# Three partial sums at later turns, and the gain row spread by one-pass products

## The chip, the core and the metric

The kernel runs on one core of one Trainium2 chip. The metric is the time of one execution on the device in microseconds (us). Three timed runs of the kernel before gave 869.16, 869.48 and 869.73 us. A profiled execution, taken separately, is what the views below show.

## What is computed

One encoder layer on a sequence of 512 tokens of width 1024, in float32: an S5 state-space branch and a gated spatial mixer run side by side and are merged by two sigmoid gates; then come attention to 256 memory tokens and a SwiGLU network.

```python
n = rms_norm(h, mix_norm_g)            # h = x
proj = n @ w_in                         # 1024 x 4608: xa, zu, zv, gate_a, gate_b
ya = s5_branch(xa, ...)                 # two scans, GLU with w_glu
yb = sgu_branch(zu, zv, ...)            # layer norm, 128 x 128 mixing per head
merged = sigmoid(gate_a) * (ya @ w_proj_a) + sigmoid(gate_b) * (yb @ w_proj_b)
h = h + merged @ w_out
h = h + memory_cross_attention(rms_norm(h), rms_norm(mem), w_q, w_k, w_v, w_xo)
h = h + (silu(rms_norm(h) @ w_gate) * (rms_norm(h) @ w_up)) @ w_down
return rms_norm(h, final_norm_g)
```

## The kernel before

**Products.** TensorE has a one-pass product for operands of the type float32r and a slower one, which shows as two matmul records, for plain float32. Nearly every matrix product uses the first: each operand is split into a high part (a cast by ScalarE, line 85) and the rest (a subtraction by VectorE, line 86), and three products, high by high, high by rest and rest by high, are added (mm3, line 401). Several large products (gate b, the queries, the SwiGLU network) are done with seven products of half-size blocks instead of eight; these need sums and differences of weight blocks.

**The plan.** All weight blocks, 512 KB each, stand in one list in the order of use. next_w (line 374) is called once for each block, at its *turn*: it starts the loads that are due up to seven turns ahead (begin, line 387; most loads are due three turns ahead, into three buffers named wraw), splits the blocks up to two turns ahead (three buffers each for whi and wlo), and hands out the block of the turn. The turns that matter here: 36 to 49 are the 14 products of gate b, 50 and 51 w_glu, 52 to 55 w_proj_a, 56 to 63 w_out, 64 on w_k.

**The partial sums.** The sums of weight blocks that the queries and w_down need later are made in device memory by transfers alone (plan_sums, line 301). Each is a pair: a copy, issued by SyncE (line 316), and two to four turns later an addition, a GpSimd transfer that adds a second block to the first (line 317). plan_sums is given the turn of each copy and the distance to its addition. The eight pairs of the queries come first; the next seven, at turns 50 to 62, are six chunks of one sum of w_down and the first chunk of another.

**What sets the order.** The kernel is built by a planner that traces the program and then orders each engine's instructions itself, by what is ready first in its own model of time. An instruction named in keep_in_program_order (in_order for short) stays behind the instruction that was traced just before it on its engine. The copies of the partial sums are held in this way; their additions are not.

**The gate stage.** Around turns 36 to 49 the tile gw holds the blocks of gate b's two halves (plan_gates, line 233). ORDER (line 230) is the order of the products (q, i), with q the number of the product and i the half: (1, 0), (1, 1), (2, 0), (2, 1), (5, 0), (6, 0), (5, 1), (7, 0), (6, 1), (4, 0), (7, 1), (3, 0), (4, 1), (3, 1). Once the block of (6, i) is split, a GpSimd transfer adds a further block of w_in to it in place (line 261); the result is the block of (4, i). Products 6, 7 and 4 of a half add up in one bank of TensorE's output memory (gx); between 7 and 4 ScalarE copies the bank out as u (kept, line 1311, line 1313), so product 4 waits for that copy. The four loads named gat (line 1452), the other gate's values, are traced after w_glu and before turn 52.

**The front.** g_row, one row of 1024 numbers on one partition, is the gain of the first norm. It is spread over 128 partitions by products with a row of ones (pg, line 638). idles (line 610) issues products of a tile of ones that nobody reads; they keep TensorE busy ahead of its first real work. row_sums squares a row of x in halves on ScalarE, rms_factor makes r from it on VectorE and GpSimd, scaled multiplies x by r and by pg, then x is transposed by TensorE (line 577) and split.

Of the kernel before, what the change touches and what calls it, by code (L numbers as in the profile page):

```python
# [9 lines left out]
F32 = mybir.dt.float32  # L10
F32R = mybir.dt.float32r
AF = mybir.ActivationFunctionType
ALU = mybir.AluOpType
# [4 lines left out]
P = 128  # L18
D = 1024
# [33 lines left out]
def hybrid_layer_kernel(  # L53
# [8 lines left out]
    nc = tc.nc  # L62
# [17 lines left out]
    def aux(name, shape=(P, 512)):  # L80
        return pa.tile(list(shape), F32, tag="aux", name=name)
# [12 lines left out]
    in_order = tc.keep_in_program_order  # L94
# [119 lines left out]
    def query_block(i, j, n):  # L214
        return block(w_q, i * KD // 2, KD // 2, 512 * n + 256 * j, 256)
# [78 lines left out]
    def down_block(i, jc, c):  # L294
        row, k = (4 * c + 2 * i, 2) if c < CHUNKS - 1 else (NF - 2 + i, 1)
        return block(w_down, row, k, 512 * (1 - jc), 512)

    def down_sum(q, c):
        return dsum[q][:, 2 * c:min(2 * c + 2, NF // 2), :]

    def plan_sums(places):


        jobs = []
        for q, first, more in ((5, (0, 0), lambda n: query_block(0, 1, n)), (7, (0, 1), lambda n: query_block(1, 1, n)),
                               (6, None, lambda n: query_block(1, 1, n)), (4, None, lambda n: query_block(1, 0, n))):
            for n in range(2):
                jobs.append((qsum[q, n], qsum[q + (-1 if q == 6 else 2), n] if first is None else query_block(*first, n),
                             more(n)))
        for q, i, jc, more in ((5, 0, 0, lambda c: down_block(0, 1, c)), (7, 0, 1, lambda c: down_block(1, 1, c)),  # L310
                               (6, 1, 1, lambda c: down_sum(5, c)), (4, 1, 0, lambda c: down_sum(6, c))):
            for c in range(CHUNKS):
                jobs.append((down_sum(q, c), down_block(i, jc, c), more(c)))
        assert len(jobs) == len(places)
        for (dst, src, more), (j, step) in zip(jobs, places):
            plan[j][1].append((0, lambda d=dst, x=src: tc.keep_in_program_order(nc.sync.dma_start(d, x))))
            plan[j + step][1].append((0, lambda d=dst, x=more: nc.gpsimd.dma_start(d, x, accum_op=ALU.add)))  # L317
# [44 lines left out]
    for i in range(4):  # L362
# [4 lines left out]
    plan_down(w_down, lambda q, c: down_tokens[0](q, c), down_plan)  # L367
    plan_units(UNITS, down_plan)

    plan_sums([(5 + 3 * i, 3) for i in range(8)] + [(50 + 2 * i, 2) for i in range(7)] +  # L370
              [(85 + 3 * i, 3) for i in range(3)] + [(122 + 5 * i, 4) for i in range(14)])
    used_w = [0]

# [22 lines left out]
    def split_w(j):  # L396
        tiles.append(plan[j][2]())
# [132 lines left out]
    ones = cp.tile([P, P], F32, name="ones")  # L530
# [10 lines left out]
    def rms_factor(ss, r=None):  # L541

        ms = np_.tile([P, 1], F32, tag="ms", name="ms", bufs=2)
        if r is None:
            r = np_.tile([P, 1], F32, tag="r", name="r", bufs=2)
        nc.vector.tensor_tensor(ms, ss[:, 0:1], ss[:, 1:2], ALU.add)
        nc.vector.tensor_scalar(ms, ms, 1.0 / D, EPS, ALU.mult, ALU.add)
        nc.gpsimd.tensor_tensor(r, ms, mhalf, ALU.pow)
        return r

    HALF = (slice(0, 512), slice(512, 1024))

    def row_sums(src, order=(0, 1)):
        ss = np_.tile([P, 2], F32, tag="ss", name="ss", bufs=2)
        for i in order:
            sum_sq(ss[:, i:i + 1], src[:, HALF[i]])
        return ss
# [13 lines left out]
    def to_feat(src, hi, lo, tsl, full=None, skip=None, part=(0, 1), behind=None):  # L571

        for q in part:
            ps = aux("ptr", (P, 4, P))
            for j in range(4):
                k = 4 * q + j
                tr = nc.tensor.transpose(ps[:, j, :], src[:, k * P:(k + 1) * P], ident)  # L577
                row_tr[0] = tr.ins
                if behind is not None:
                    in_order(tr)  # L580
            if q != skip:
                turned[:] = split(hi[:, 4 * q:4 * q + 4, tsl], lo[:, 4 * q:4 * q + 4, tsl], ps)
            if full is not None:
                nc.scalar.copy(full[:, 4 * q:4 * q + 4, tsl], ps)
        if behind is not None:
            long_idle(*behind)
# [8 lines left out]
    def slot(tag, shape, dt, name):  # L595
        return sp.tile(list(shape), dt, tag=tag, name=name)
# [13 lines left out]
    def idles(n):  # L610
        for i in range(n):
            in_order(nc.tensor.matmul(idle, ones, ones, start=True, stop=True))

    idles(8)
    warm = np_.tile([P, 1], F32, tag="ms", name="warm", bufs=2)
    nc.scalar.activation(warm, mhalf, AF.Square)

# [2 lines left out]
    g_row = np_.tile([1, D], F32, tag="gain", name="g_row", bufs=2)  # L620
# [13 lines left out]
    def first_rows():  # L634

        pg = [aux("pg") for i in range(2)]
        for i in range(2):
            in_order(nc.tensor.matmul(pg[i], ones[0:1, :], g_row[:, HALF[i]], start=True, stop=True))
        idles(1)
        def scaled(t, q, r, g):  # L640
            return in_order(nc.vector.scalar_tensor_tensor(
                xt[:, t, HALF[q]], xt[:, t, HALF[q]], r, g, ALU.mult, ALU.mult))

        def gain_copy(q):
            in_order(nc.vector.tensor_copy(g_mix[:, HALF[q]], pg[q]) if q == 0 else
                     nc.scalar.copy(g_mix[:, HALF[q]], pg[q]))

        def turn(t, q):
            to_feat(xt[:, t, :], xn_hi, xn_lo, slice(t * P, t * P + P), part=(q,))

        def parts(j):
            raw = plan[j][3].pop("raw")
            hi = wp.tile([P, 2, 512], F32R, tag="hi", name="whi", bufs=3)
            lo = wp.tile([P, 2, 512], F32R, tag="lo", name="wlo", bufs=3)
            tiles.append((hi, lo))
            high = lambda q: in_order(nc.scalar.copy(hi[:, q], raw[:, q]))
            low = lambda q: in_order(nc.vector.tensor_tensor(lo[:, q], raw[:, q], hi[:, q].bitcast(F32), ALU.subtract))
            return high, low

        pinned[0] = True  # L660
        r = rms_factor(row_sums(xt[:, 0, :], (1, 0)))
        scaled(0, 0, r, pg[0])
        high, low = parts(0)
        high(0)
        low(0)
        gain_copy(0)
        turn(0, 0)
        idles(3)
        scaled(0, 1, r, pg[1])
        r = rms_factor(row_sums(xt[:, 1, :]))  # L670
        high(1)
        low(1)
        high, low = parts(1)
        wide = slice(0, 2)
        high(wide)
        gain_copy(1)
        scaled(1, 0, r, g_mix[:, HALF[0]])
        low(wide)
        turn(1, 0)
        turn(0, 1)  # L680
        scaled(1, 1, r, g_mix[:, HALF[1]])
        split_w(2)
        ss = row_sums(xt[:, 2, :])
        r = rms_factor(ss)
        turn(1, 1)
        turned1 = [row_tr[0]]
        pinned[0] = False
        with tc.issue_after(turned[0].ins):
            ss = row_sums(xt[:, 3, :])
        for t in range(2, NT):  # L690
            with tc.issue_after(turned[1].ins) if t > 2 else nullcontext():
                for i in range(2):
                    sc = nc.vector.scalar_tensor_tensor(
                        xt[:, t, HALF[i]], xt[:, t, HALF[i]], r, g_mix[:, HALF[i]], ALU.mult, ALU.mult)
            r = rms_factor(ss) if t == 2 else None
            turn(t, 0)
            turned1.append(row_tr[0])
            turn(t, 1)
        return turned1

    turned1 = first_rows()
    last_row = [x.ins for x in turned]

# [1331 lines left out]
```

## Time and profile before

| | |
|---|---|
| median of three timed runs | 869.48 us |
| lowest and highest | 869.16 and 869.73 us |
| profiled execution, its time | 867.14 us |
| its span, first to last instruction | 865.4 us |
| mean granted TensorE clock in it | 0.996 |
| TensorE products / weight loads, busy | 853.9 us (99%) / 761.9 us (88%) |
| VectorE, ScalarE, GpSimd busy | 648.2, 475.1, 103.5 us |
| moved by transfers | 155.40 MB |

In the views PE is TensorE's products, PEld its weight loads, DVE VectorE, ACT ScalarE, POOL GpSimd, SP SyncE; POOLq, SPq and the like are the queues in which an engine issues transfers. L404 is line 404. A group "out<-in" names the tile written and the tile read. Times are microseconds from the start of the span. Products overlap, and their ends are modelled, so the busy time of PE alone doesn't say that it is at its peak; a stop shows as a gap between starts.

### The profile page before, as it was taken

The numbers are of one execution on the slowest core, as the hardware profiler recorded it, in microseconds if no ns is written. First come the engines' busy times: TensorE is split into PE (matmuls) and PEld (weight loads), VectorE is DVE, ScalarE is ACT, GpSimd is POOL, SyncE is SP. The second block draws the span as 40 slices with busy tenths as digits, with TensorE's granted clock in tenths as the row PEclk, the third lists the DMA queues.
The fourth block names the chain that finished last, engine by engine and source line by source line (L and its number), as shares of the span: only waits on it lengthen the run. The fifth ranks groups of instructions, "written<-read, shape, count | busy, mean of one in ns | idle before, by whom it ended". The sixth has DMA issues, their size and how long they took to land.

```text
span 865.4 us, 14842 instructions
## 1 busy us (share of the span) xinstructions
PE 853.9 (99%) x5898; PEld 761.9 (88%) x5898; DVE 648.2 (75%) x890; ACT 475.1 (55%) x703; POOL 103.5 (12%) x157
## 2 busy tenths in 40 slices
PE   9999999999999899999999999999999999999996
PEld 6788888878889888889899888999999999988885
DVE  6699589957947658669658646767877768899876
ACT  6645774377436534557547544645545555656664
POOL 1001144100611010110010001001111111000000
PEclk9999999999999999999999999999999999999999
DMA  8559279645638586944687144557799789686641
GB/s 260 159 144 240 81 204 267 147 122 162 167 98 226 136 224 202 287 116 169 200 269 216 68 145 105 146 140 177 172 224 230 204 208 240 178 243 203 196 158 48
DMA packets 110135, 155.40 MB, mean 180 GB/s; under 512 B 8985, under 2 KB 77105, under 8 KB 110002
## 3 DMA queue, kind: packets, MB, share of 16 engines
q1 hardware_dynamic: 91762, 128.27, 45.3%
q0 software_dynamic: 18016, 25.66, 18.4%
q8 instruction: 46, 0.75, 0.3%
q10 hardware_dynamic: 288, 0.52, 0.2%
q14 instruction: 23, 0.19, 0.1%
HBM read 148.70 MB, written 37.20 MB: 215 GB/s over the span
## 4 chain that ended last, share of the span: by engine, by line
PE 96%; ACT 1%; DVE 1%; issue 1%; POOLq 0%; POOL 0%; ACTq 0%
PE pf L404 25%; PE pt L404 18%; PE px L1304 13%; PE dx L404 6%; PE pq L1304 6%; PE dq L404 3%; PE pv L1304 3%; PE gx L1304 3%; PE qx L1304 3%; PE dv L404 2%; PE ptr L577 1%; PE psc L404 1%; PE gq L1304 1%; PE po L404 1%; PE py L1093 1%; PE qq L1304 1%
## 5 line engine op out<-in xcount | busy, mean ns | idle before, releaser
L85 ACT CAST whi<-wraw 128x1024 fp32r<-128x1024 f32 x132 | 135.8, 1029 | 143.3 <-PE pf L404 37.2
L86 DVE TENSOR_TENSOR wlo<-wraw,whi 128x1024 fp32r<-128x1024 f32 x132 | 157.5, 1194 | 66.0 <-ACT whi L85 65.7
L404 PE MATMUL pf<-xn,whi 128*128 128x512 f32 x320 | 100.4, 393 | 0.0
L1304 PE MATMUL px<-fn,whi 128*128 128x256 f32 x480 | 83.3, 276 | 0.0
L1304 PEld LDWEIGHTS px<-fn,whi 128*128 128x128 f32 x480 | 72.5, 188 | 0.2
L404 PEld LDWEIGHTS pf<-xn,whi 128*128 128x128 f32 x320 | 59.6, 188 | 12.6 <-issue 0.5
L85 ACT CAST whi<-b 128x1024 fp32r<-128x1024 f32 x40 | 42.1, 1054 | 51.5 <-PE px L1304 26.3
L86 DVE TENSOR_TENSOR wlo<-b,whi 128x1024 fp32r<-128x1024 f32 x40 | 48.9, 1224 | 27.9 <-ACT whi L85 27.9
L1304 PE MATMUL px<-fn,wlo 128*128 128x256 f32 x240 | 66.4, 277 | 0.0
L404 PE MATMUL pf<-xn,wlo 128*128 128x512 f32 x160 | 62.9, 393 | 0.0
L1304 PE MATMUL pq<-s,whi 128*128 128x256 f32 x320 | 55.0, 276 | 0.0
L404 PE MATMUL dx<-whi,s 128*128 128x512 f32 x170 | 53.0, 390 | 0.0
L86 DVE TENSOR_TENSOR wlo<-t,whi 128x1024 fp32r<-128x1024 f32 x30 | 36.7, 1225 | 19.3 <-ACT whi L85 19.3
L85 ACT CAST whi<-t 128x1024 fp32r<-128x1024 f32 x30 | 31.6, 1052 | 35.2 <-PE pv L1304 12.6
L1304 PEld LDWEIGHTS pq<-s,whi 128*128 128x128 f32 x320 | 48.2, 188 | 0.0
L1304 PEld LDWEIGHTS px<-fn,wlo 128*128 128x128 f32 x240 | 45.1, 188 | 0.0
L1304 PE MATMUL pq<-s,wlo 128*128 128x256 f32 x160 | 44.2, 276 | 0.0
L404 PE MATMUL pt<-whi,xn 128*128 128x512 f32 x120 | 40.1, 402 | 0.0
L404 PEld LDWEIGHTS dx<-whi,s 128*128 128x128 f32 x170 | 31.8, 188 | 6.7 <-DVE s L86 0.3
L317 POOL DMA_DIRECT2D dsum<-in_w_down_dram x12 | 13.3, 1108 | 192.1 <-DMA dsum<-in_w_down_dram 192.1
L404 PEld LDWEIGHTS pf<-xn,wlo 128*128 128x128 f32 x160 | 30.1, 188 | 6.1 <-issue 0.2
L404 PE MATMUL dx<-wlo,s 128*128 128x512 f32 x85 | 33.0, 390 | 0.1
(485 smaller groups left out, 2340.0 us busy)
## 6 DMA issues: line engine op xcount, KB each, us to landing
wraw<-in_w_in_dram SPq DMA_DIRECT2D x34, 512.0 KB, 6.1
dsum<-in_w_down_dram SPq DMA_DIRECT2D x20, 512.0 KB, 6.4
wraw<-dsum SPq DMA_DIRECT2D x20, 512.0 KB, 3.7
b<-in_w_gate_dram SPq DMA_DIRECT2D x15, 512.0 KB, 5.1
b<-in_w_up_dram SPq DMA_DIRECT2D x15, 512.0 KB, 5.2
wraw<-in_w_down_dram SPq DMA_DIRECT2D x15, 512.0 KB, 4.7
dsum<-in_w_down_dram POOLq DMA_DIRECT2D x10, 512.0 KB, 7.3
dsum<-dsum POOLq DMA_DIRECT2D x10, 512.0 KB, 7.1
```

Source lines behind the costliest of these rows:

```text
L85: hi = nc.scalar.copy(dst_hi, src)
L86: lo = nc.vector.tensor_tensor(dst_lo, src, dst_hi.bitcast(F32), ALU.subtract)
L317: plan[j + step][1].append((0, lambda d=dst, x=more: nc.gpsimd.dma_start(d, x, accum_op=ALU.add)))
L404: last_mm[0] = nc.tensor.matmul(ps, a[x], b[y], start=start and i == 0, stop=stop and i == 2, skip_group_check=free)
L577: tr = nc.tensor.transpose(ps[:, j, :], src[:, k * P:(k + 1) * P], ident)
L1093: in_order(nc.tensor.matmul(ps[64 * j:64 * j + 64, :], a, b, start=g % 4 == k == 0, stop=k == 2, tile_position=(0, 64 * j), skip_group_che ...
L1304: nc.tensor.matmul(ps[:, j, :], a[x], b[y], start=start and j == k == i == 0, stop=k == 3 and i == 2, skip_group_check=True)
```

## The change

Three edits. The first three of the seven pairs at turns 50 to 62 get later turns: 53, 54 and 55 in place of 50, 52 and 54; the distance to the addition stays two. The gain row is split into a high part and the rest, on ScalarE and VectorE, in a new tile g_parts, whose third row holds ones, and four one-pass products spread it in place of two plain ones. The idle products in front go from eight to five, those behind the gain row from one to four.

```diff
-    plan_sums([(5 + 3 * i, 3) for i in range(8)] + [(50 + 2 * i, 2) for i in range(7)] +
+    plan_sums([(5 + 3 * i, 3) for i in range(8)] + [(j, 2) for j in (53, 54, 55, 56, 58, 60, 62)] +
               [(85 + 3 * i, 3) for i in range(3)] + [(122 + 5 * i, 4) for i in range(14)])
...
-    idles(8)
+    idles(5)
...
         pg = [aux("pg") for i in range(2)]
+        g_parts = slot("D", (1, 3, D), F32R, "g_parts")
+        one_row = g_parts[:, 2, 0:P]
+        in_order(nc.vector.tensor_copy(one_row, ones[0:1, :]))
         for i in range(2):
-            in_order(nc.tensor.matmul(pg[i], ones[0:1, :], g_row[:, HALF[i]], start=True, stop=True))
-        idles(1)
+            in_order((nc.scalar.copy, nc.vector.tensor_copy)[i](g_parts[:, 0, HALF[i]], g_row[:, HALF[i]]))
+        for i in range(2):
+            in_order(nc.vector.tensor_tensor(g_parts[:, 1, HALF[i]], g_row[:, HALF[i]],
+                                             g_parts[:, 0, HALF[i]].bitcast(F32), ALU.subtract))
+        for j in range(2):
+            for i in range(2):
+                in_order(nc.tensor.matmul(pg[i], one_row, g_parts[:, j, HALF[i]], start=j == 0, stop=j == 1))
+        idles(4)
```

## The prediction

> **What bounds the kernel now.** I read the page's chain that ended last, then the waits of TensorE, then the chain and the engines' timelines around the one long wait, and at last the first 12 us. The chain says which engine to argue about:
>
> ```profile
> span 865.4 us, 14842 instructions
> PE 96%; ACT 1%; DVE 1%; issue 1%; POOLq 0%; POOL 0%; ACTq 0%
> ```
>
> TensorE is the path for 96% of the span. A change that leaves the number of its big products alone can gain only where TensorE stands still or runs slowly. The waits of TensorE (who waited for whom: total, times, longest) name the places:
>
> ```profile
> PE gx L1304 <- ACT u L1313: 2.4, 1, 2.4
> PE pt L483 <- ACT whi L656: 1.0, 1, 1.0
> ```
>
> Beside these only the start and 0.2 us stand in that view. The short one is in the first 11 us, the long one in the gate stage. The chain there, in order of time (start, length, what):
>
> ```profile
> 278.88 5.50 PE gx L1304 x47
> 284.38 0.02 issue
> ...
> 286.39 0.49 ACT u L1313
> ...
> 286.93 4.46 PE gx L1304 x24
> ...
> 291.81 2.86 PE gx L1304 x24
> ```
>
> TensorE stops at 284.38 and goes on at 286.93: 2.55 us lost. The next 24 products take 4.46 us where 24 equal ones take 2.86. The stretches of the trace (columns: from and to, length, busy time and count of PE, PEld, DVE, ACT, POOL, then the granted clock, DMA share, GB/s) say why:
>
> ```profile
> 287.00:292.00 5.00, 5.00 (x30) 5.00 (x30) 3.17 (x4) 2.69 (x4) 0.00 (x0) 0.66 0.24 79
> 292.00:303.00 11.00, 11.00 (x95) 10.96 (x94) 8.59 (x11) 6.23 (x10) 0.00 (x0) 1.00 0.45 151
> 10.00:12.00 2.00, 1.91 (x8) 1.50 (x9) 1.93 (x3) 1.47 (x3) 0.55 (x1) 1.00 1.04 409
> ```
>
> After the stop the granted clock was 0.66 over 5 us, then 1.00 again: 5 x 0.34 = 1.7 us of full-speed work lost. The place costs 2.55 + 1.7 = 4.25 us, 0.5% of the span. (The last row is the stretch behind the 1.0 us wait: 1.00.)
>
> What ends the wait? ScalarE, VectorE, GpSimd and SyncE there (start, length, engine, line, operation; in brackets the idle time before and its releaser):
>
> ```profile
> 277.32 0.58 ACT L1404 COPY u<-gx 128x512 f32<-128x512 f32 x1
> 284.40 1.99 ACT L85 CAST whi<-gw 128x1024 fp32r<-128x1024 f32 x2 [6.51 <-PE gx L1304]
> 270.65 2.40 DVE L86 TENSOR_TENSOR wlo<-gw,whi 128x1024 fp32r<-128x1024 f32 x2
> 277.44 1.23 DVE L86 TENSOR_TENSOR wlo<-gw,whi 128x1024 fp32r<-128x1024 f32 x1 [0.39 <-ACT whi L85]
> 272.63 1.20 POOL L317 DMA_DIRECT2D dsum<-in_w_down_dram  x1 [31.20 <-DMA dsum<-in_w_down_dram]
> 273.99 1.35 POOL L261 DMA_DIRECT2D gw<-in_w_in_dram  x1 [0.16 <-issue]
> 278.96 1.28 POOL L261 DMA_DIRECT2D gw<-in_w_in_dram  x1 [3.62 <-DVE wlo L86]
> 265.00 1.49 SPq L1452 DMA_DIRECT2D gat<-gad  x1
> 266.53 0.60 SPq L316 DMA_DIRECT2D dsum<-in_w_down_dram  x1
> 296.97 0.37 SPq L141 DMA_DIRECT2D wraw<-in_w_proj_a_dram  x1
> 297.39 0.58 SPq L316 DMA_DIRECT2D dsum<-in_w_down_dram  x1
> DMA to landing us min/median/max: 7.9/9.1/10.3
> DMA to landing us min/median/max: 6.1/7.9/10.3
> ```
>
> (The last two: the two GpSimd transfers of line 261, then these and the one of line 267 together.) ScalarE does nothing from 277.90 to 284.40, then casts two weight tiles, and only then copies u, for which TensorE waits. The releaser named is a product that had ended long before. A wait for several events is put down to the one that the profile saw last, so it was another, and a transfer fits. Tiles are cast in the plan's order, and the first of these two is that of (4, 0), the product in which TensorE resumes, and the transfer that completes it is line 261's first: issued at 273.99, 10.3 us in flight, landed at 284.3. It went out that late, and took 10.3 us where its sister took 7.9, because a partial sum for w_down (line 317) stood ahead of it on GpSimd: 1.20 us at 272.63, for a transfer of equal size ahead of its own. That sum belongs to the SyncE transfer at 266.53.
>
> **The change part by part.** *The places.* The first three of seven pairs move, from the turns 50, 52, 54 to 53, 54, 55; the other four stay. A pair is a plain copy on SyncE, held behind the transfer traced before it, and an addition on GpSimd two turns on, not held. Counting turns, the copy of turn 52 is traced right behind the four loads of gat: it is the one at 266.53, 1.53 us behind the last gat. The copy of turn 50 is traced behind the first load for w_proj_a: the one at 297.39. In the new places the three are traced behind the loads of turns 55, 56 and 57, the last one for w_proj_a and the first two for w_out:
>
> ```profile
> 299.44 6.02 SPq L141 DMA_DIRECT2D wraw<-in_w_proj_a_dram  x3
> 310.39 0.37 SPq L141 DMA_DIRECT2D wraw<-in_w_out_dram  x1
> 315.82 0.37 SPq L141 DMA_DIRECT2D wraw<-in_w_out_dram  x1
> 318.06 0.56 SPq L316 DMA_DIRECT2D dsum<-in_w_down_dram  x1
> 326.74 2.10 SPq L141 DMA_DIRECT2D wraw<-in_w_out_dram  x2
> ```
>
> So, on before's scale, at about 305.5, 310.8 and 316.2, with the unmoved fourth still at 318.06. The count stays: seven copies, seven additions, no load more or less. The second pair moves on SyncE past the rest of the gate's loads, w_glu's and w_proj_a's; on GpSimd past both transfers of line 261.
>
> What goes: the 1.20 us and the wait ahead of line 261. Its first transfer needs the split of the tile that it overwrites, in the plan's order the first of the two subtractions at 270.65, so 270.65 + 1.2 = 271.9; the second of line 261 started 0.3 us behind its own split (277.44 + 1.23 = 278.67, 278.96). So about 272.2, where it was 273.99. In flight: 6.1 at the least and 10.3 at the most in the rows above, and I take 7.9, its sister's: landing at 280.1 (278.3 to 282.5). Then the two casts and the copy of u. The second cast needs a buffer free that the product (7, 0) reads, until 281.7 (278.88 + 24 of 47 products of 5.50 us): 281.8 to 282.8, u to 283.4, and TensorE wants it at 284.38. The wait is gone with 1 us to spare; if the landing is at 282.5, the copy is over at 282.5 + 1.99 + 0.49 = 285.0 and 0.6 us is left of the wait. What is late next is line 261's second transfer, unmoved, 278.96 + 7.9 = 286.9; its tile is used three products later, at 284.38 + 3 x 2.86 = 293.0, and cast and subtraction (1.0 and 1.23) leave it 3.8 us. Gain of the wait: 2.55 (1.9 to 2.55). The 1.0 us wait in the first 11 us left the granted clock at 1.00, so I take the 1.7 to go with the stop; at the least it stays. Gain of the place: **4.2 us**, between 1.9 and 4.25. That w_in's load behind the moved copy lands sooner gains nothing: TensorE works without a break from 278.88 to 284.38, and the tile is not the one it waits for.
>
> What comes: three copies and additions among the loads for w_out. That is cost nothing because those loads run far ahead: loads 3 and 4 for w_out go out at 326.74, and TensorE comes to the third block at 335.44 + 2 x 5.44 = 346.3 (a block is 24 of the 75 products in 17.01 us, rows below). If that cover is gone the price is the slower rival's.
>
> *The front.* Before's rows:
>
> ```profile
> 0.74 0.35 SPq L621 DMA_DIRECT2D g_row<-in_mix_norm_g_dram  x1
> 1.06 3.78 PE L612 MATMUL idle<-ones 128*128 128x128 f32 x16 [1.06 <-DVE level L880]
> 3.66 0.63 ACT L537 ACTIVATE sq<-xt 128x512 f32<-128x512 f32 x1 [1.01 <-DMA xt<-in_x_dram]
> 4.77 2.05 PE L638 MATMUL pg<-g_row,ones 1*128 1x512 f32 x4
> 5.02 0.16 DVE L546 TENSOR_TENSOR ms<-ss 128x1 f32<-128x1 f32 x1 [2.89 <-ACT sq L537]
> 6.07 0.75 DVE L641 SCALAR_TENSOR_TENSOR xt<-xt,r,pg 128x512 f32<-128x512 f32 x1 [0.58 <-POOL r L548]
> 7.66 0.68 DVE L645 COPY g_mix<-pg 128x512 f32<-128x512 f32 x1
> ```
>
> Two products that run as four passes (2.05 us) become four that run as one pass each, over the same 512 columns, and I price a pass alike; six of 16 front passes go and six come behind. On ScalarE comes one copy of 512 columns, on VectorE a small copy, one of 512 and two subtractions: 0.6 (the copy at 277.32), and 0.16 (the smallest, as at 5.02) + 3 x 0.7 = 2.3 us (the copy at 7.66). The first scaling at 6.07 waited for r, not for the gain row: earlier rows gain nothing. VectorE has 2.89 us free before 5.02, ScalarE 1.01 before 3.66; the copies start when g_row lands. No row shows that. It left at 0.74, with the half of x that ScalarE squares at 3.66, and has 4 KB: about 3.0 is my estimate. Then ScalarE is done by 3.6 and the subtractions by 5.0: hidden, barely. If g_row lands at 3.66, the square and all behind it come 0.6 us later. I take 0.1 us lost, between 0 and 0.6. [...] A late full pace is bounded by half of TensorE's time up to the scaling, and there it isn't the path: inside the same 0.6.
>
> **Sum.** -4.2 + 0.1 = -4.1 us. The profiled execution took 867.14 us (span 865.4): 863.0 for its like. It lies 2.3 us under the median of the timed runs, 869.48, which spread over 0.57 us; I take the difference as equal in both, and predict 865.4 us. A measurement can tell about 0.2%, 1.7 us, from no change.
>
> **The rivals.** (1) *The clock's dip isn't the stop's.* Then only the wait goes: 2.5 - 0.1, 867.1 us. For it: the dip lies in a stretch in which TensorE is busy throughout (287 to 292). Against: that stretch is right behind the only long stop, and the next is at 1.00. Chance 0.12. [...]
>
> (2) *The change doesn't do what it says.* The additions on GpSimd aren't held: one of another pair could again stand ahead of line 261, or the copies slip forward as turn 52's did. Then nothing is gained: 869.48 + 0.1 = 869.6 us, or some 868 if half of the wait is left. Against: the new places hang behind the load of turn 55, which SyncE sends after 299.44, and every addition needs its copy landed. Chance 0.14.
>
> (3) *Slower: the loads for w_out starve.* Four copies now stand on SyncE between 305.5 and 318.06, ahead of the loads at 326.74.
>
> ```profile
> DMA to landing us min/median/max: 3.8/6.0/9.8
> wraw<-in_w_out_dram SPq DMA_DIRECT2D x8, 512.0 KB, 4.5
> 335.44 17.01 PE pt L404 x75
> ```
>
> If the four are served one behind the other at 6.0 us, they end at 329.5 and nothing is late. At 9.8 each they end at 344.7; the third load needs 4.5, a cast and a subtraction 2.3 more: 351.5, 5.2 us after 346.3, and after such a stop another 1.7 of clock. Net 5.2 + 1.7 - 4.1 = 2.8 us slower: 872.3. It decides from (346.3 - 305.5 - 6.8) / 4 = 8.5 us a copy. For it: GpSimd's additions share the DMA engines. Against: 6.0 is measured with them. Chance 0.08 for this and whatever else is slower.
>
> **How the numbers follow.** Forecast 0.66 (its own range 864.6 to 866.8), rivals 0.12, 0.14, 0.08. Low end: the whole 4.25 and the runs' spread of 0.57 besides, 864.6. High end: rival 1 with a front that loses 0.6 and that spread's half, 867.9. Some 0.78 lies inside. Faster by over 0.2%: 0.66 + 0.12 = 0.78; within: 0.14; slower: 0.08.
>
> **What would show it.** In after's profile: no copy of dsum between the gat loads and the first w_proj_a load; line 261's first transfer near 272 and under 9 us in flight; no wait of gx for u; granted clock 1.00 from 254 to 303; w_proj_b's stage before it unchanged within 0.3 us. It is wrong if line 261 starts no earlier, if TensorE waits in w_out, or if the first scaling comes after 6.7.

## The result and the profile after

The changed kernel takes 863.75 us (median of six runs, 863.64 to 863.97); the kernel before, in six runs (the three given ahead are among them), 869.88 us (869.16 to 870.82). The ratio is 0.993, 95% interval 0.9917 to 0.9942. That is 6.1 us faster where 4.1 were forecast, and 0.85 us below the low end of the range. Later comparisons, in which the runs of before spread further, gave 0.9944 (0.9924 to 0.9963) and 0.9953 (0.9938 to 0.9968) for the same kernel at 863.69 and 863.78 us: the changed kernel's own time is the same each time, before's is not. Where that comes from is the main find.

Line numbers of the changed kernel behind the front are up by nine: the gate's product is L1313, the copy of u L1322, the product for the gain row L647, the scaling L650.

The page's head and its chain by engine, after:

```profile
span 862.2 us, 14843 instructions
PE 96%; DVE 1%; ACT 1%; issue 1%; POOLq 0%; POOL 0%; ACTq 0%
```

The span is 3.2 us shorter; the profiled execution took 863.97 us (before's 867.14). So the two profiles differ by 3.2 us and the timed medians by 6.1. The waits of TensorE, after (total, times, longest):

```profile
PE idle L612 <- DVE level L889: 1.1, 1, 1.1
PE pt L483 <- ACT whi L665: 0.3, 1, 0.3
PE pf L404 <- DVE yb_lo L86: 0.2, 1, 0.2
```

The wait for u, 2.4 us before, is gone. The chain in the gate stage and the stretches, after, as they were shown of before:

```profile
279.93 8.46 PE gx L1313 x72
...
288.63 2.88 PE gx L1313 x24
...
299.62 5.46 PE pf L404 x24
```

```profile
284.00:287.00 3.00, 3.00 (x28) 3.00 (x27) 2.29 (x3) 2.06 (x5) 0.00 (x0) 1.00 0.55 86
287.00:292.00 5.00, 5.00 (x44) 5.00 (x43) 3.19 (x4) 2.59 (x4) 0.00 (x0) 1.00 0.32 105
303.00:324.00 21.00, 21.00 (x95) 17.38 (x94) 13.09 (x15) 8.65 (x13) 2.29 (x2) 1.00 0.91 261
324.00:346.00 22.00, 22.00 (x99) 18.22 (x98) 17.97 (x28) 9.69 (x15) 3.03 (x5) 1.00 0.90 271
```

72 products run in one piece, the granted clock is 1.00, and behind it, in w_out, TensorE is busy for all 43 us although the DMA engines are now 0.90 to 0.91 busy. What the helpers did, after:

```profile
271.70 2.39 DVE L86 TENSOR_TENSOR wlo<-gw,whi 128x1024 fp32r<-128x1024 f32 x2
274.07 1.37 POOL L261 DMA_DIRECT2D gw<-in_w_in_dram  x1 [31.15 <-issue]
DMA to landing us min/median/max: 5.9/5.9/5.9
280.11 1.05 ACT L85 CAST whi<-gw 128x1024 fp32r<-128x1024 f32 x1 [1.17 <-DMA gw<-in_w_in_dram]
282.98 1.05 ACT L85 CAST whi<-gw 128x1024 fp32r<-128x1024 f32 x1 [1.82 <-PE gx L1313]
283.93 0.58 ACT L1322 COPY u<-gx 128x512 f32<-128x512 f32 x1
302.35 0.61 SPq L316 DMA_DIRECT2D dsum<-in_w_down_dram  x1
307.65 0.58 SPq L316 DMA_DIRECT2D dsum<-in_w_down_dram  x1
```

No partial sum stands ahead of line 261 on GpSimd; its transfer lands 5.9 us after its issue (10.3 before) and the cast takes the tile at once, this time with the transfer named as releaser. The third line is that of line 261's two transfers.

The chain of the whole span, before and then after, gives where the first long run of 85 products and the first one behind the gate stage begin (start, length, what):

```profile
41.97 19.32 PE pf L404 x85
...
302.78 32.66 PE pf L404 x144
```

```profile
43.03 19.32 PE pf L404 x85
...
299.62 32.66 PE pf L404 x144
```

At the first mark the profile after is 1.06 us *late*, at the second 3.16 us early. Between the two marks 4.22 us are won, which is the 4.25 of the prediction's first section; in front of them 1.06 us are lost. By the profiles the change is 4.2 - 1.06 = 3.2 us better; the timed runs say about 3 more, and that must be in what differs between one execution of before and another.

### The profile page after: what moved, and what is told of

It is laid out like the page before. It is cut to its first block, busy times and chain, and to the rows that moved or that the text cites. A ratio compares the mean times of both kernels' runs of the same rounds, so it can differ in the third digit from the quotient of the medians.

```text
span 862.2 us, 14843 instructions
## 1 busy us (share of the span) xinstructions
PE 853.9 (99%) x5898; PEld 762.6 (88%) x5898; DVE 649.5 (75%) x894; ACT 475.8 (55%) x704; POOL 103.6 (12%) x157
## 4 chain that ended last, share of the span: by engine, by line
PE 96%; DVE 1%; ACT 1%; issue 1%; POOLq 0%; POOL 0%; ACTq 0%
PE pf L404 25%; PE pt L404 18%; PE px L1313 13%; PE dx L404 6%; PE pq L1313 6%; PE dq L404 3%; PE pv L1313 3%; PE gx L1313 3%; PE qx L1313 3%; PE dv L404 2%; PE ptr L577 1%; PE psc L404 1%; PE po L404 1%; PE py L1102 1%; PE qq L1313 1%; PE gq L1313 1%
## 5 line engine op out<-in xcount | busy, mean ns | idle before, releaser
L1313 PE MATMUL px<-fn,whi 128*128 128x256 f32 x480 | 83.3, 277 | 0.0
L1313 PEld LDWEIGHTS px<-fn,whi 128*128 128x128 f32 x480 | 72.7, 188 | 0.2
L1313 PE MATMUL px<-fn,wlo 128*128 128x256 f32 x240 | 66.5, 277 | 0.0
L1313 PE MATMUL pq<-s,whi 128*128 128x256 f32 x320 | 55.0, 277 | 0.0
L1313 PEld LDWEIGHTS pq<-s,whi 128*128 128x128 f32 x320 | 48.3, 188 | 0.0
L1313 PEld LDWEIGHTS px<-fn,wlo 128*128 128x128 f32 x240 | 45.1, 188 | 0.0
L1313 PE MATMUL pq<-s,wlo 128*128 128x256 f32 x160 | 44.3, 277 | 0.0
```

The costliest lines, as they stand in the source:

```text
L1313: nc.tensor.matmul(ps[:, j, :], a[x], b[y], start=start and j == k == i == 0, stop=k == 3 and i == 2, skip_group_check=True)
```

## The experiments

The theory: the gate stage behaves as forecast, and the rest is the front. In most executions TensorE's clock comes to full late, and then the plain products of before hold the first transposes, which the one-pass products don't. The rivals: the timed median is constantly 2.3 us above a profile (the prediction's reading), or the fewer idle products in front do it.

All runs, with when the granted clock first came to full by the trace's clock record, the start of the first four transposes and of the 85 products in the one profiled execution of each (us from the start of its span; but for before's first profile that execution is also one of the runs):

| kernel | median (lowest to highest), runs | ratio to before (95%) | full clock | transposes | 85 products | wait for u |
|---|---|---|---|---|---|---|
| before, first profile | 869.48 (869.16 to 869.73), 3 | | 4.96 | 7.08 | 41.97 | 2.4 |
| after | 863.75 (863.64 to 863.97), 6 | 0.993 (0.9917 to 0.9942) | 11.69 | 7.36 | 43.03 | none |
| before_again | 867.77 (865.18 to 870.30), 12 | 1.0001 (0.9986 to 1.0017) | 4.69, lost at 8.10, again 14.93 | 6.99 | 43.95 | 1.8 |
| places_only | 865.61 (865.09 to 866.02), 6 | 0.997 (0.9958 to 0.9982) | 13.55 | 9.07 | 44.85 | none |
| front_only | 867.87 (865.71 to 868.30), 12 | 0.9992 (0.9982 to 1.0002) | 10.14 | 7.36 | 42.72 | 2.4 |
| idles_only | 869.48 (867.71 to 870.54), 11 | 1.0016 (1.0007 to 1.0026) | 12.42 | 9.06 | 44.44 | 2.4 |
| split_only | 867.12 (866.05 to 869.85), 12 | 0.9989 (0.9973 to 1.0005) | 9.75 | 7.36 | 42.75 | 4.4 |
| stop_filled | 866.57 (865.84 to 868.68), 12 | 0.9972 (0.9956 to 0.9988) | 9.92 | 7.36 | 42.73 | 0.2 |
| stop_one_row | 867.39 (866.34 to 869.64), 12 | 0.999 (0.9972 to 1.0007) | 9.46 | 7.36 | 42.74 | none |
| after_again | 863.69 (863.60 to 863.91), 6 | 0.9944 (0.9924 to 0.9963) | 10.60 | 7.36 | 42.69 | none |
| second_pair | 864.85 (863.03 to 865.69), 9 | 0.9958 (0.9944 to 0.9973) | 5.57 | 7.38 | 42.26 | none |
| after_third | 863.78 (863.67 to 864.03), 6 | 0.9953 (0.9938 to 0.9968) | 9.43 | 7.49 | 42.87 | none |
| full_rows | 862.97 (862.78 to 863.16), 6 | 0.9944 (0.9927 to 0.9961) | 4.90 | 6.77 | 41.72 | none |

before_again, places_only, front_only and idles_only share 30 runs of before, 867.6 us (864.65 to 870.21); split_only, stop_filled, stop_one_row and after_again (the changed kernel unaltered) share 29, 869.05 us (864.62 to 872.84). The last three share 14, 867.6 us (864.49 to 870.12). For after_again a gain of 3.5 to 4.5 us had been expected; it was 5.4 against that median.

**before_again**, the kernel before, unaltered.

> The kernel before, unchanged, for a second profiled execution. The change gained 6.1 us in the timed runs, but the two profiles differ by only 3.2 us, because the first profile of before is 2.7 us faster than its own timed runs. Theory A (front): in most executions of before TensorE's clock is released late at the start, as it was not in the first profile; then this profile shows the first products of the zv stage (the chain piece at 13.57 in the first profile) about 2.7 us later, the gate stage again with a stop of 2.55 us and 1.7 us of clock, and a time of 869.5 to 870.5. Theory B (gate stage): the front is as in the first profile and the stop at the gate is longer, 4 us or more, or followed by two dips of the clock. Theory C: neither, the 2.7 us lie somewhere else or outside the span.

Before doesn't have one time: its runs lie around 865, 867.5 and 870 us, and five of the 29 above 871. Of theory A the late front came and its gate stage didn't: this profiled execution had a shorter wait for u and no half clock behind it, but at the start it did this (stretches, columns as before: the third number from the end is the granted clock):

```profile
4.80:8.00 3.20, 3.20 (x17) 1.96 (x16) 2.30 (x7) 0.99 (x2) 0.55 (x1) 1.00 0.92 341
8.20:11.40 3.20, 2.69 (x6) 1.67 (x6) 2.99 (x7) 3.18 (x8) 0.55 (x1) 0.50 1.05 415
11.60:14.80 3.20, 3.20 (x12) 2.61 (x11) 0.88 (x1) 0.13 (x1) 0.00 (x0) 0.50 1.00 238
15.00:18.00 3.00, 3.00 (x16) 2.32 (x15) 2.71 (x4) 2.94 (x7) 0.00 (x0) 1.00 0.69 148
```

The full clock came, went for two stretches of 3.4 us each, and came again: 43.95 in the table, 2.0 us behind the first profile of the same kernel. The front is not the same in every execution.

**places_only**, the turns alone, with before's front:

```diff
+    plan_sums([(5 + 3 * i, 3) for i in range(8)] + [(j, 2) for j in (53, 54, 55, 56, 58, 60, 62)] +
```

> Before with the three later turns alone. Theory A: the stop and the dip go, 4.25 us, and the front stays late: 865.6 us against 869.9 (ratio 0.995). Theory B: the whole gain is here, 863.8 us (0.993). In both the profile shows no wait of TensorE for u and line 261's first transfer under 7 us in flight.

865.61 us, as theory A had it, though the ratio is 0.997 (0.9958 to 0.9982), since the runs of before beside it spread; no wait for u, and line 261's transfers took 5.9 and 6.0 us. All six runs lie within 1 us, above all of after's: 1.9 us between the medians, for the front edit. The front in before's first profile, then in this one (the last row is the chain's):

```profile
7.08 0.60 PE L577 MATMUL ptr<-ident,xt 128*128 128x128 f32 x4
```

```profile
5.55 0.55 POOL L548 TENSOR_TENSOR r<-ms,mhalf 128x1 f32<-128x1 f32 x1 [3.71 <-DVE ms L547]
4.77 3.78 PE L638 MATMUL pg<-g_row,ones 1*128 1x512 f32 x4
6.95 0.75 DVE L641 SCALAR_TENSOR_TENSOR xt<-xt,r,pg 128x512 f32<-128x512 f32 x1 [1.36 <-POOL r L548]
9.07 1.06 PE L577 MATMUL ptr<-ident,xt 128*128 128x128 f32 x4
44.85 19.32 PE pf L404 x85
```

This is the front that the first profile of before didn't show. The gain row's products took 3.78 us where they took 2.05, and the four transposes behind them on TensorE 1.06 where they took 0.60: about half pace. The transposes start 1.99 us later than in before's profile and the 85 products 2.88. (The releaser named for the scaling is r, but r was done at 5.55 + 0.55 = 6.10 and the scaling began at 6.95: what it waited for was the gain row's product.) So after's front, 1.06 us late against one profile, is 1.82 us early against this one.

**front_only**, the split row and the moved idle products, with before's turns.

```diff
-    plan_sums([(5 + 3 * i, 3) for i in range(8)] + [(j, 2) for j in (53, 54, 55, 56, 58, 60, 62)] +
+    plan_sums([(5 + 3 * i, 3) for i in range(8)] + [(50 + 2 * i, 2) for i in range(7)] +
```

> Before with the split gain row and the moved idle products alone, the seven pairs at their old turns. Theory A: the front's share, 1.8 us: 868.1 us against 869.9 (0.998), the gate stage with its stop as before. Theory B: nothing or 0.1 us lost: 869.9 to 870.0.

The wait for u stays at 2.4 us and the front comes to 42.72, but the ratio, 0.9992, can't be told from 1. The front's gain is in the trace and is not seen as a ratio here. Three of the twelve runs lie at 865.71 to 866.24 and nine at 867.16 to 868.30. After's 863.7 plus the stop of 2.5 is 866.2, plus 1.7 for the clock 867.9: the two groups. That working is mine and not shown: a clock record exists for the profiled executions alone, and the mean clocks of the other runs (0.997 for the early three, 0.995 to 0.999 for the nine) don't tell the groups apart.

**idles_only** and **split_only** take the front edit apart. The first has the idle products moved and before's two plain products, the second the split row and before's idle products.

> Before with the idle products moved alone (five in front, four behind), the gain row still spread by two plain products. Theory A with the idle products as the cause: 1.8 us gained, 868.1. Theory A with the earlier, split gain row as the cause: nothing or a loss, 869.9 to 871. Theory B: 869.9.

> Before with the gain row split and spread by four one-pass products, but the idle products as they were (eight in front, one behind), turns as in before. Theory A' with the passes as the cause: at half clock the four passes take 2.0 us in place of 3.7, but begin only at 4.8 us: the first scaling comes about 0.9 us later than in front_only when the clock is late, 866 to 869. Rival, the idle products are the cause: no better than before.

idles_only, then split_only:

```profile
3.49 3.78 PE L638 MATMUL pg<-g_row,ones 1*128 1x512 f32 x4
6.09 0.75 DVE L641 SCALAR_TENSOR_TENSOR xt<-xt,r,pg 128x512 f32<-128x512 f32 x1 [0.55 <-POOL r L548]
9.06 1.06 PE L577 MATMUL ptr<-ident,xt 128*128 128x128 f32 x4
44.44 19.32 PE pf L404 x85
```

```profile
4.77 2.07 PE L647 MATMUL pg<-g_parts 1*128 1x512 f32 x4
7.36 1.09 PE L577 MATMUL ptr<-ident,xt 128*128 128x128 f32 x4
42.75 19.32 PE pf L404 x85
PE gx L1313 <- ACT u L1322: 4.4, 1, 4.4
DMA to landing us min/median/max: 10.0/10.4/10.8
```

Moving the idle products alone leaves the transposes at 9.06 and makes the kernel 0.16% slower (0.07 to 0.26%). Its scaling begins at 6.09, as early as in before's profile (6.07), and still the transposes come at 9.06: what they wait for is not the scaling but the products ahead of them on TensorE, which are as many in either order (18 records of idle products and the row's four). The one-pass products alone bring them to 7.36, as early as with both; the 1.71 us against places_only's 9.07 are the difference of the row's products, 3.78 and 2.07. I had expected split_only's first scaling 0.9 us behind front_only's; it is 0.3 (6.53 and 6.21), and the 85 products 0.03. So the rival of the idle products falls, and of the front edit the one-pass products are all that gains. This rests on the traces, one execution of each; in time split_only can't be told from before. The last two lines show besides that the stop is not a constant: with the sum's transfer ahead, line 261's two took 10.0 and 10.8 us, and the stop was 4.4.

**second_pair** moves one of the seven pairs by one turn and nothing else:

```diff
-    plan_sums([(5 + 3 * i, 3) for i in range(8)] + [(50 + 2 * i, 2) for i in range(7)] +
+    plan_sums([(5 + 3 * i, 3) for i in range(8)] + [(j, 2) for j in (50, 53, 54, 56, 58, 60, 62)] +
```

> The kernel before with one place moved alone: the second pair's turn 52 becomes 53 and the third's 54 stays, so only the pair whose copy lay behind the gat loads comes later by one turn (turns 50, 53, 54, 56, 58, 60, 62). If the length of the gate stage's stop hangs on that one pair's copy and the GpSimd transfer behind its addition, the copy still lies behind the gat loads, and the stop stays at 1.8 to 4.4 us: the time is the kernel before's within 0.2%. If instead all that matters is how many GpSimd transfers are in flight beside line 261's, the stop becomes shorter and the time falls by 1 to 2 us.

My first branch was wrong: one turn is enough. Turn 53 is traced behind the last load for w_proj_a, not behind the gat loads, so the moved copy goes out at 301.58 (the one at 293.46 is the unmoved first pair's), with no addition ahead of line 261:

```profile
273.29 1.37 POOL L261 DMA_DIRECT2D gw<-in_w_in_dram  x1 [31.35 <-issue]
DMA to landing us min/median/max: 6.0/6.1/6.2
```

No wait for u is left, and the time falls to 864.85, as in places_only or more. The prediction's cause, this pair's copy at 266.53, is so shown by itself; the other two moves of the change give nothing that can be seen. The nine runs also show the two fronts side by side: four at 863.03 to 863.43 (among them the profiled one, whose gain row products took 2.35 us) and five at 864.85 to 865.69. The six runs of after_third beside them, 863.67 to 864.03, lie between: by the medians its front loses 0.6 us against the early group and gains 1.7 against the late one. That the groups are an early and a late full clock is shown for the profiled run alone. After's own full clock came late in all three of its profiles, at 9.43 to 11.69.

**stop_filled** and **stop_one_row** keep the stop of front_only and give TensorE ten products that nobody reads in it, on 128 rows or on one:

```diff
+        if n == 9:
+            fill = aux("fill")
+            for _ in range(10):
+                in_order(nc.tensor.matmul(fill, xn_hi[0:P, 0, 0:P], xn_hi[0:P, 0, :], start=True, stop=True))
```

> The front's part of the change alone (turns as in before, so the stop at the gate stays), with ten products of 512 columns on all 128 rows issued into the stop; their result is read by nobody. Theory A': the wait stays (TensorE resumes with the product (4, 0) 2.5 us after (6, 1)), but the clock never dips: one group, 865.7 to 866.4, where front_only had 865.7 to 868.3 in two groups (one with the dip, 1.7 us later). Rival: the dip has nothing to do with TensorE standing still: two groups as in front_only.

> As stop_filled, but the ten products use one row of the array only, in the same time. If products on one row count as activity: one group, 865.7 to 866.4, as stop_filled. If they don't: two groups as front_only, 865.7 to 868.3, most of them at 867.2 or above. The gain row's products at the front are such one-row products, so this tells whether they keep the clock.

```profile
285.08 2.44 PE L1443 MATMUL fill<-xn 128*128 128x512 f32 x10
PE gx L1313 <- ACT u L1322: 0.2, 1, 0.2
```

```profile
285.15 2.58 PE L1443 MATMUL fill<-xn 1*128 1x512 f32 x10
```

The two fill the same 2.5 us. With 128 rows ten of twelve runs lie at 865.84 to 866.75, with mean granted clocks of 0.998 or 0.999. With one row six lie at 866.34 to 866.94, with 0.997 to 0.999, and six at 867.84 to 869.64, with 0.994 to 0.997. Both profiled executions show 1.00 throughout the gate stage. The two intervals of the ratios overlap, so this points to products on one row counting little for the clock, and doesn't settle it. That a stop filled on all rows leaves fewer executions in the late group (two of twelve, where front_only has nine) speaks for the 1.7 us being the stop's. A further sign is in before_again's rows above: TensorE is busy for all of 4.80 to 8.00, 1.98 us of it from 4.75 on with the one-row products of the gain row, and at 8.10 the full clock is lost. But before's first profile, busy for all of 4.96 to 8.37 with 2.05 us of the same products from 4.77 on, kept it.

**after_third** and **full_rows** test that from the other side. after_third is the changed kernel unaltered; full_rows has the row in a tile of 128 rows, zero but for the first, so that the four products run on all 128 rows:

```diff
-        g_parts = slot("D", (1, 3, D), F32R, "g_parts")
+        g_parts = slot("D", (P, 3, D), F32R, "g_parts")
...
+        in_order(nc.vector.memset(one_row.bitcast(F32), 0.0))
+        in_order(nc.vector.tensor_copy(one_row[0:1], ones[0:1, :]))
+        in_order(nc.vector.memset(g_parts[:, 0, :].bitcast(F32), 0.0))
+        in_order(nc.gpsimd.memset(g_parts[:, 1, :].bitcast(F32), 0.0))
+        top = g_parts[0:1]
```

(The casts and subtractions then write into top.)

> The changed kernel unaltered, beside the one with full rows on the same chip: 863.7 within 0.3, no wait for u in the gate stage, and the full clock late (some 10 to 13 us after the start).

> The changed kernel with the four gain-row products on all 128 rows: the split row lies in the first row of a tile that is otherwise zero, and the ones in the first row of a 128 x 128 tile of zeros; the result is the same sum. If products on one row do not count as activity for the clock (as the ten products in the stop suggest), these four now count: the full clock comes in an earlier window, the first transposes and products run less time at half pace, and w's first unit (the long pf group at the start) ends its chain 0.3 to 1.0 us earlier than the 42.7 to 43.0 of the changed kernel: 862.7 to 863.4. If only the zeroing (VectorE and GpSimd) comes in the way of the row's copies, 863.7 to 864.5. Rival: the rows make no difference to the clock, 863.7 within 0.2.

```profile
3.57 1.82 PE L651 MATMUL pg<-g_parts 128*128 128x512 f32 x4
5.96 0.75 DVE L654 SCALAR_TENSOR_TENSOR xt<-xt,r,pg 128x512 f32<-128x512 f32 x1 [0.55 <-POOL r L548]
6.77 0.66 PE L577 MATMUL ptr<-ident,xt 128*128 128x128 f32 x4 [0.48 <-DVE xt L654]
41.72 19.30 PE pf L404 x85
```

862.97 us beside 863.78: 0.8 us, and no run of the one reaches a run of the other. The full clock came at 4.90, in after_third at 9.43. After's first profile compares better: counted back by two steps of 3.41 us from the 11.69 at which it did, its clock could have changed at 4.86 (my estimate), nearly at full_rows's 4.90, and it didn't. The transposes run at full pace (0.66 us for four, 1.06 in after) and now wait for their data, 0.48 us, no longer for TensorE's queue. This is the fastest version measured here, and six runs within 0.4 us show no trace of a late clock.

## Why the prediction was right and wrong

*Right: the gate stage, with its cause.* The stop and the half clock behind it are both gone, 4.22 us between two marks for 4.2 forecast. The copies go out at 302.35, 307.65 and 313.07, 3.1 to 3.2 us ahead of the 305.5, 310.8 and 316.2 forecast, which is the time won by then. The landing came at 274.07 + 5.9 = 280.0, or 278.9 with the 1.06 us of the front taken off, where 280.1 was forecast. u is copied by 283.93 + 0.58 = 284.5, and TensorE comes to the product that needs it after 48 of the 72 products from 279.93, at 285.6: 1.1 us to spare, as forecast. Two of its sizes were off: line 261 began at 274.07, or 273.0 with the 1.06 us of the front taken off, where 272.2 was forecast, and the flight was 5.9 us, not 7.9. The start is 1.1 us behind the end of the first of the two subtractions and within 0.03 us of the end of the second (271.70 + 2.39 = 274.09); the row names no releaser, so which of them it waited for stays open. Neither size mattered, since the cast that came last waited for the buffer, as forecast, and not for the landing.

*Rival 1, the clock's dip isn't the stop's:* against it speak the profile after and stop_filled. But the stop doesn't always bring it: front_only's profile has a wait of 2.4 us and 1.00 behind it, idles_only's one of 2.4 us and 0.61 over 288 to 292. Of the five profiled executions with an unfilled stop three have the half clock behind it (the last section has what TensorE worked in each). So the 1.7 us are lost in a part of the executions; the forecast took them as sure, and that the one profile it had was of this kind is luck.

*Rival 2, the change doesn't do what it says:* refuted; the three copies went out where they were placed, and no addition stood ahead of line 261.

*Rival 3, w_out starves:* refuted; the DMA engines did fill, from 0.68 busy before to 0.90 after between 324 and 346, and TensorE never waited.

*Wrong: the front.* The step that failed is "A late full pace is bounded by half of TensorE's time up to the scaling, and there it isn't the path: inside the same 0.6." With it fell "I take the difference as equal in both". What is on the path is TensorE's own queue in front of the first transposes, not the scaling: at half pace the two plain products, 3.78 us together, keep the transposes until 9.07, the four one-pass products, 2.07 us, until 7.36. So a second term was mis-sized, "I price a pass alike": the four one-pass products took little more than half of what the four records of the plain ones took at the same pace, and this is the gain that the forecast put at nothing. It looked free since before's one profile had the full clock early, 4.96 us after the start by the trace's clock record; after's had it at 11.69 and places_only's at 13.55. In its profile the change loses 1.06 us in front, and the median of before's runs, which were not like its profile, wins 1.8 (44.85 to 43.03). If the three timed runs had both the late front and the half clock at the stop, the sum is -4.25 - 1.8 = -6.05 us from 869.48, or 863.4; measured were 863.75. For the profiles 867.14 - 4.2 + 1.06 = 864.0, where 863.97 were measured, only adds up what was read from the two.

The 2.3 us between before's profile and its median were thus no overhead of timing: after's profiled execution (863.97) is one of its six timed runs (863.64 to 863.97). By places_only's profile they were the front of another execution. The six runs of before beside after, with the three that were given among them, all fell in the late group around 870. By the two later ratios, against runs from all of before's groups, the change is worth 4 to 5 us, against that group 6.

Open stays how often before's front has an early full clock (its runs have a mean clock each and no record over time, and the two effects overlap in their times), and why nine of front_only's twelve runs lie in the later of its two groups.

## What to carry over

Where one profile and the timed median differ by more than the runs' spread, look for a stage that can go two ways before calling it an offset: a changed kernel may have only one of them. In a front that starts at half pace, count TensorE's whole queue up to its first useful product at that pace, and make the products there one-pass (2.07 us in place of 3.78 here) and, as full_rows suggests (862.97 us beside 863.78), on all rows. A GpSimd transfer that overwrites a tile in use paid here for a transfer just ahead of it twice, in its start (1.0 us) and, more, in its flight (10.3 us in place of 5.9); moving one pair by one turn was the whole gain of the places.

## What the runs showed of the hardware

- The clock changed in steps of one length (the windows of the expectations): in before's record the half clock lies from 288.26 to 291.67, 3.41 us, and the 283.30 us from 4.96 to 288.26 are 83 times 3.413; in before_again's two such steps follow each other, from 8.10 to 14.93. Where the steps lie differs between executions: before's two profiles had the full clock first at 4.96 and at 4.69, only the second lost it again in front, and their 85 products began at 41.97 and 43.95.
- Whether a stop cost the clock went with how much TensorE worked in one such step. Counted on in steps of 3.413 us from the changes on record, the step that holds most of the stop had 1.33 us of work in before, 1.45 in idles_only and none in split_only, and the next one ran at half clock (0.50 in before; 0.61 in idles_only and 0.71 in split_only over 288 to 292, which holds most of it); with 1.89 us in before_again and 1.98 in front_only the full clock stayed, 1.00 from 284 to 292. For these two, where no change follows in the gate stage, the place of the step is an estimate. These are five executions; where between 1.45 and 1.89 the border lies, none of them shows. The length of the wait doesn't tell them apart: it was 2.4 us in before, idles_only and front_only. The steps of before (the stop's and the next), then of front_only; then the stop's alone in idles_only, split_only and before_again:

```profile
284.85:288.26 3.41, 1.33 (x11) 1.33 (x12) 2.78 (x3) 3.41 (x5) 0.00 (x0) 1.00 0.35 56
288.26:291.67 3.41, 3.41 (x19) 3.41 (x18) 1.91 (x3) 1.10 (x3) 0.00 (x0) 0.50 0.25 79
```

```profile
283.21:286.62 3.41, 1.98 (x18) 1.78 (x16) 0.53 (x1) 1.61 (x2) 0.00 (x0) 1.00 1.18 187
286.62:290.03 3.41, 2.49 (x20) 2.49 (x21) 3.41 (x4) 2.94 (x5) 0.00 (x0) 1.00 0.02 4
```

```profile
285.49:288.90 3.41, 1.45 (x13) 1.25 (x12) 1.04 (x1) 2.12 (x3) 0.00 (x0) 1.00 0.94 150
286.23:289.64 3.41, 0.00 (x0) 0.00 (x0) 1.42 (x2) 2.50 (x4) 0.00 (x0) 1.00 0.58 91
284.58:288.00 3.42, 1.89 (x17) 1.69 (x15) 1.20 (x2) 2.28 (x3) 0.00 (x0) 1.00 1.04 179
```

- The profile's clock column reads 1.00 before the first change on record: in before the idle products at the start run 16 in 3.78 us, and six like ones at 7.51 take 0.83 us, though the column reads 1.00 for both. At a kernel's start the pace is read from the length of like instructions: four transposes took 0.60 to 0.66 us or 1.06 to 1.09.
- The gain row's two plain products took 2.05 us in before, with the full clock from 4.96 on, and 3.78 at half pace, in places_only and idles_only; four one-pass products over the same columns took 2.07 at half pace, in after, front_only and split_only.
- Line 261's GpSimd transfers landed 5.8 to 6.2 us after their issue with nothing just ahead of them (six profiles, of after, after_again, after_third, places_only, second_pair and full_rows). With a partial sum's transfer shortly before (before, before_again, front_only, idles_only, split_only, stop_filled), the first of the two took 10.0 to 10.8 us and the second 7.8 to 10.0.
